# Row-major attention and mixing weights halved by DMA in a two-layer encoder

## The chip, the cores and the metric

The kernel runs on one core of one Trainium2 chip. The metric is the device time of one execution in microseconds (us), as the median of several runs. A core has five engines with a queue each: TensorE (PE, matrix products into PSUM banks), VectorE (DVE), ScalarE (ACT), GpSimd (POOL) and SyncE (SP, which here only issues DMAs). A queue is worked off in order; an instruction that waits for another engine holds up all behind it.

## The reference

Two layers on 512 tokens of width 1024, all in float32. Each layer mixes tokens in two ways side by side and then runs a gated MLP:

```python
h = rmsnorm(x, g_mix[l]); z = h @ w_in[l]
q, k, v, x_rec, gate = jnp.split(z, [512, 1024, 1536, 2048], axis=-1)
att = neighbourhood_attention(q, k, v, rel_bias[l])    # 8 heads of 64, tokens on an 8 x 64 grid
xc = depthwise_conv(x_rec, ...)                         # width 4
rec_f = rg_lru(xc, ..., reverse=False); rec_b = rg_lru(xc, ..., reverse=True)
rec = (rec_f + rec_b) * gelu(gate, approximate=True)
x = x + concat([rmsnorm(att, g_att[l]), rmsnorm(rec, g_rec[l])]) @ w_out[l]
u_act, u_lin = split(rmsnorm(x, g_ffn[l]) @ w_up[l])
x = x + (gelu(depthwise_conv(u_act, ...)) * u_lin) @ w_down[l]
```

A query at grid column c sees all 8 rows and a window of 16 columns, with a learned bias per head. `rg_lru` makes two gates r and i by 64-wide block products and sigmoids, a = exp(-8 r softplus(-lam)), and scans h = a h + sqrt(1 - a^2) i x over the tokens. A last rmsnorm ends the program.

## The kernel before

Activations lie transposed: 128 channels on the partitions, 512 tokens along them. Each weight is read from memory once, in chunks of 128 x 1024 (eight 128 x 128 blocks, 512 KB), in the order that `weight_plan` lists. Every operand of these products is split into a rounded high half and a low half, and `mm3` (L187 to L190) issues three products: high by high, low by high, high by low. A column of `w_in` (128 outputs) is eight blocks, 24 matmuls of 512 columns.

A weight chunk passes three steps. `load_to` has SP load it into `raw` (2 buffers). `split_to` has ACT copy it rounded to `hi` (L171, 4 buffers) and DVE subtract, `lo = raw - hi` (L172, 4 buffers). `chunk` hands it to the products and calls the two others for chunks further on (3 ahead for the split, 6 for the load).

The mixing stage of a layer starts with the recurrent input columns, a group of four banks (`xr`). Then the string `MIX` (L43) sets the order in which the program's steps are written, and with it TensorE's order: `q`, `k`, `v`, `g` followed by a number are the four columns of queries, keys, values and the gate branch (an `a` or `b` behind it is a half of one); `c` is the convolution of a channel tile; `t` the recurrent gates of a tile, with exponentials, a square root and the two scans (`lru_gates`, L469); `S`, `T` and `P` are scores and softmax, transposes of the weights, and products with the values, each for half the columns of a pair of heads, so numbers 0 to 7; `u` transposes values to token order and copies their halves, shifted by half a tile, into two `edge` tiles (POOL, L564); `o` and `n` are output products and norms. A scheduler sets the order of the other engines: by its own estimate of when things are ready, with what stands under `urgent()` first.

Queries, keys and values are stored column by column of the grid (`by_column`), so DVE writes or reads them in strides when it evacuates a bank (L528, L536, L547). `query_tile` (L509) keeps two tiles per pair with zeros from POOL. The gate branch computes its GeLU by hand, ACT square, three DVE steps, ACT tanh (`gate_tile`, L573), within the step that makes the column. PSUM has eight banks: three for columns (`ps_mm`), two for scores, two for transposes, one for products (`ps_o`).

After the stage come the output products and the MLP: per tile two columns of `w_up`, a convolution and a GeLU from ACT's table (L771), then `w_down`.

## Time and profile before

| what | value |
|---|---|
| three runs | 1230.93 us median, 1230.6 to 1231.04 |
| profiled execution | 1230.33 us, its span 1228.5 us |
| PE busy | 1201.5 us (98%) |
| DVE busy | 791.6 us (64%) |
| ACT busy | 488.0 us (40%) |
| POOL busy | 46.3 us (4%) |
| granted TensorE clock | 0.998 of full |

The span counts from the first instruction to the last; busy time is the union of an engine's instructions. Matmuls overlap, and their ends are modelled, so PE's share says less than its steps from one matmul to the next. By the names in the timeline the mixing stages lie at about 26 to 218 us and 631 to 823 us; MLP parts fill the rest.

### The profile page before, as it was taken

How to read it: one execution, taken by the hardware profiler on the slowest of the kernel's cores; microseconds unless marked ns; L12 is line 12 of the kernel's file. 1: busy time of each engine (PE TensorE's matmuls, PEld its weight loads, DVE VectorE, ACT ScalarE, POOL GpSimd, SP SyncE). 2: the span in 40 equal slices, each digit the busy share in tenths (PEclk: the TensorE clock that was granted, in tenths of full speed). 3: DMA queues.
4: the chain of work that ended last, by engine and by line, in shares of the span. 5: the costliest groups of instructions: out<-in, count | busy, mean ns of one | idle time of the engine just before them, and what ended most of it. 6: DMA issues, size and time to landing. Idle time of an engine off the chain costs nothing.

```text
span 1228.5 us, 14279 instructions
## 1 busy us (share of the span) xinstructions
PE 1201.5 (98%) x5566; PEld 991.2 (81%) x5566; DVE 791.6 (64%) x1257; ACT 488.0 (40%) x717; POOL 46.3 (4%) x88
## 2 busy tenths in 40 slices
PE   9999999999999999999999999999999999999997
PEld 7777778888888888888887777788888888888886
DVE  8999876865544455553659998677555255565454
ACT  6687534433221232332429765344323212223220
POOL 2001010000000000000010011100000000000000
PEclk9999999999999999999999999999999999999999
DMA  7222213223223223233222221142332322322322
GB/s 239 81 69 93 84 35 103 90 99 103 91 98 103 87 101 103 88 102 103 86 86 77 77 86 52 35 137 87 103 93 96 103 91 98 103 87 101 103 69 69
DMA packets 34355, 114.06 MB, mean 93 GB/s; under 512 B 3825, under 2 KB 7025, under 8 KB 34289
## 3 DMA queue, kind: packets, MB, share of 16 engines
q1 hardware_dynamic: 34144, 113.17, 28.1%
q8 instruction: 43, 0.70, 0.2%
q14 instruction: 24, 0.19, 0.0%
q10 hardware_dynamic: 144, 0.00, 0.0%
HBM read 111.06 MB, written 2.10 MB: 92 GB/s over the span
## 4 chain that ended last, share of the span: by engine, by line
PE 78%; DVE 11%; ACT 4%; issue 2%; DMA 1%; POOL 0%; POOLq 0%; DVEq 0%; ACTq 0%
PE dn L188 7%; PE dn L190 7%; PE dn L189 7%; PE pl L188 6%; PE pa L188 6%; PE pa L189 6%; PE pl L189 6%; PE pa L190 6%; PE pl L190 6%; PE out L188 2%; PE out L190 2%; PE out L189 2%; DVE lo L172 2%; PE up L188 1%; PE up L190 1%
## 5 line engine op out<-in xcount | busy, mean ns | idle before, releaser
L171 ACT ACTIVATE hi<-raw 128x1024 fp32r<-128x1024 f32 (+1 forms) x205 | 216.3, 1055 | 452.9 <-PE dn L189 156.6
L172 DVE TENSOR_TENSOR lo<-raw,hi 128x1024 fp32r<-128x1024 f32 (+1 forms) x205 | 249.6, 1218 | 142.9 <-ACT hi L171 142.4
L763 DVE TENSOR_TENSOR ua<-pa,g_ffn_rb 128x512 f32<-128x512 f32 x44 | 30.4, 691 | 112.9 <-PE pa L190 112.9
L771 ACT ACTIVATE uc<-uc,cols 128x512 f32<-128x512 f32 x48 | 34.8, 724 | 129.7 <-DVE uc L769 129.6
L772 DVE TENSOR_TENSOR uc<-pl,uc 128x512 f32<-128x512 f32 x44 | 30.4, 691 | 73.5 <-PE pl L190 72.0
L740 DVE TENSOR_TENSOR dns<-dn,g_ffn_rb 128x512 f32<-128x512 f32 x30 | 20.4, 689 | 29.4 <-PE dn L190 29.4
L769 DVE SCALAR_TENSOR_TENSOR uc<-ua,cols,uc 128x511 f32<-128x511 f32 x48 | 36.0, 751 | 1.5
L767 DVE SCALAR_TENSOR_TENSOR uc<-ua,cols,uc 128x511 f32<-128x511 f32 x48 | 35.8, 745 | 0.1
L628 ACT ACTIVATE prob<-prob,mx 128x192 f32<-128x192 f32 (+1 forms) x64 | 27.5, 431 | 12.0 <-DVE mx L626 11.9
L615 PEld LDWEIGHTS s<-k,q 128*128 128x128 f32 x128 | 19.6, 190 | 8.8 <-issue 4.2
L188 PE MATMUL out<-atth,hi 128*128 128x512 f32 x64 | 26.1, 407 | 0.4 <-ACT atth L684 0.4
L615 PE MATMUL s<-k,q 128*128 128x192 f32 (+1 forms) x128 | 23.2, 324 | 3.2 <-DVE mx L622 1.4
L190 PE MATMUL out<-atth,lo 128*128 128x512 f32 x64 | 25.4, 397 | 0.0
L189 PE MATMUL out<-attl,hi 128*128 128x512 f32 x64 | 25.3, 396 | 0.0
L766 DVE TENSOR_SCALAR uc<-ua,cols 128x512 f32<-128x512 f32 x48 | 23.4, 487 | 1.5
L517 POOL MEMSET q<- 64x256 f32 x32 | 10.0, 311 | 367.4 <-PE dn L189 366.1
L679 DVE COPY att<-o 64x256 f32<-64x256 f32 x32 | 19.6, 612 | 4.6 <-PE o L190 4.1
L528 DVE TENSOR_TENSOR q<-qps,g_mix_rb 64x256 f32<-64x256 f32 x32 | 20.6, 644 | 0.4
L741 DVE TENSOR_TENSOR x<-x,dns 128x512 f32<-128x512 f32 x30 | 20.1, 687 | 0.4
L622 DVE CUSTOM_DVE_ANT_0 prob<-s,bias 128x192 f32<-128x192 f32 (+1 forms) x64 | 18.2, 338 | 1.8 <-PE pte L649 0.6
L564 POOL CAST edge<-vh 64x384 fp32r<-64x384 f32 x16 | 9.4, 591 | 254.5 <-ACT vh L559 254.0
L458 DVE SCALAR_TENSOR_TENSOR xc<-xrs,cols,xc 128x511 f32<-128x511 f32 (+1 forms) x24 | 17.9, 747 | 0.4
(930 smaller groups left out, 3547.4 us busy)
## 6 DMA issues: line engine op xcount, KB each, us to landing
raw<-in_w SPq DMA_DIRECT2D x203, 512.0 KB, 3.5
x<-in_x SPq DMA_DIRECT2D x8, 256.0 KB, 5.1
out_y<-out SPq DMA_DIRECT2D x8, 256.0 KB, 2.3
bias<-in_bias SPq DMA_DIRECT2D x8, 224.0 KB, 2.5
raw<-in_w SPq DMA_DIRECT2D x2, 256.0 KB, 3.1
cols<-in_cols SPq DMA_DIRECT2D x1, 164.0 KB, 5.0
cols<-in_cols ACTq DMA_DIRECT2D x1, 4.0 KB, 3.0
```

What stands on the lines that cost most here:

```text
L171: nc.scalar.activation(hi[:, sl], raw[:, sl], AF.Copy)
L172: nc.vector.tensor_tensor(out=lo[:, sl], in0=raw[:, sl], in1=f32(hi[:, sl]), op=ALU.subtract)
L188: nc.tensor.matmul(ps, a[0], b[0], start=start, stop=False)
L189: nc.tensor.matmul(ps, a[0], b[1], start=False, stop=False)
L190: nc.tensor.matmul(ps, a[1], b[0], start=False, stop=stop)
L615: nc.tensor.matmul(ps[:, o:o + ROWS * w], qt[:, b % 4 * P:(b % 4 + 1) * P], kt[:, ROWS * kc0:ROWS * (kc0 + w)], start=True, stop=True)
L628: nc.scalar.activation(pr[b], pr[b], AF.Exp, bias=mx[:, b % 4:b % 4 + 1], accum_out=sm[:, b % 4:b % 4 + 1])
L763: nc.vector.tensor_tensor(out=ua, in0=pa, in1=rbf[0], op=ALU.mult)
L767: nc.vector.scalar_tensor_tensor(out=c[:, 1:], in0=ua[:, :T - 1], scalar=w[0], in1=c[:, 1:], op0=ALU.mult, op1=ALU.add)
L769: nc.vector.scalar_tensor_tensor(out=c[:, :T - 1], in0=ua[:, 1:], scalar=w[2], in1=c[:, :T - 1], op0=ALU.mult, op1=ALU.add)
L771: nc.scalar.activation(c, c, AF.Gelu_apprx_tanh, bias=col("conv_ffn_b", j, l))
L772: nc.vector.tensor_tensor(out=c, in0=pl_, in1=c, op=ALU.mult)
```

## The change

Four things change together.

- **Layout.** Queries, keys and values stay in row order within groups of 8 grid columns (`by_group`), the bias table is laid out to match on the host, and the scores' moving operand is read through a pattern of runs of 8. The two query tiles per pair become one constant tile `q_pair` whose zeros are written once.
- **Weights.** For the mixing stage's columns and gate chunks (`by_dma`), POOL issues a DMA that rounds the weights into `hi`; ACT writes `lo = -hi`; POOL issues a second DMA that adds the weights to `lo`. Loads run at most 3 chunks ahead and splits 2. The recurrent input columns, `w_out` and the MLP keep the old way.
- **Order.** `MIX` is written anew: a pair's gates, convolution and scans come with its heads instead of all at the front, gates in two halves inside the keys' column, values before scores. A gate chunk now holds one tile (half width, 256 KB), so a layer's stage has 20 chunks by DMA, where 18 stood.
- **Gate branch.** One table GeLU on ACT, in a step `e` of its own, and one product.

`p_w2` goes to one buffer, and the softmax steps stand under `urgent()` one by one.

```diff
@@ -40,9 +40,11 @@
 
 
 
-MIX = ("q0 c0 c1 k0 t0 k1 q1 c2 t1 q2 k2 c3 t2 k3 q3 S0 v0a T0 t3 v0b g0a v1a S1 u0 P0 "
...
+
+MIX = ("q0 c0 k0a t0a k0b t0b v0a S0 v0b S1 g0a c1 u0 g0b T0 q1a q1b P0 T1 c2 k1a t1a k1b P1 t1b "
+       "v1a e0 S2 v1b S3 g1a u1 c3 g1b T2 q2a q2b P2 T3 k2a t2a k2b P3 t2b "
...
 IN_TILE = {"q": 0, "k": 4, "v": 8, "g": 16}
 
 
...
@@ -59,9 +61,8 @@
 
         pairs("w_in", 0, 8, [12, 13, 14, 15])
         for step in MIX:
-            if step in ("t0", "t0a", "t2", "t2a"):
-                t = int(step[1])
-                plan.append(("gate", l, [(t + a, dg) for a in range(2) for dg in range(4)]))
+            if step[0] == "t" and step[-1] != "b":
+                plan.append(("gate", l, [(int(step[1]), dg) for dg in range(4)]))
             elif step[0] in IN_TILE and step[-1] != "b":
                 column("w_in", IN_TILE[step[0]] + int(step[1]))
         for m in range(0, 8, 2):
...
@@ -142,16 +143,31 @@
         return tc.high_priority(offset=level * URGENT) if level else ExitStack()
 
 
-    raws, halves = {}, {}
+    raws, highs, halves = {}, {}, {}
     state = {"load": 0, "split": 0, "use": 0}
     AHEAD_LOAD, AHEAD_SPLIT = 6, 3
 
     def pieces(i):
         return (slice(0, 1024),) if i else (slice(0, 512), slice(512, 1024))
+
+    def width(i):
+        return P * len(plan[i][2])
+
+    def by_dma(i):
+
+        w, _, bs = plan[i]
+        return w == "gate" or w == "w_in" and bs[0][1] != 12
 
     def load_to(n):
         while state["load"] < min(n, len(plan)):
             i = state["load"]
+            if by_dma(i):
+                if i > state["use"] + 3:
+                    return
+                highs[i] = p_hi.tile([P, 1024], F32R, tag="hi", name=f"hi{i}")
+                nc.gpsimd.dma_start(highs[i][:, :width(i)], w_d[i][:, :width(i)])
+                state["load"] += 1
+                continue
             raws[i] = p_raw.tile([P, 1024], F32, tag="raw", name=f"raw{i}")
             for n, sl in enumerate(pieces(i)):
                 nc.sync.dma_start(raws[i][:, sl], w_d[i][:, sl])
...
@@ -162,7 +178,19 @@
     def split_to(n):
         while state["split"] < min(n, len(plan)):
             i = state["split"]
+            if by_dma(i) and i > state["use"] + 2:
+                return
             load_to(i + 1)
+            if i in highs:
+                hi = highs.pop(i)
+                lo = p_lo.tile([P, 1024], F32R, tag="lo", name=f"lo{i}")
+                with urgent(1):
+                    ws = slice(0, width(i))
+                    nc.scalar.activation(lo[:, ws], f32(hi[:, ws]), AF.Copy, scale=-1.0)
+                    nc.gpsimd.dma_start(lo[:, ws], w_d[i][:, ws], accum_op=ALU.add)
+                halves[i] = (hi, lo)
+                state["split"] += 1
+                continue
             raw = raws.pop(i)
             hi = p_hi.tile([P, 1024], F32R, tag="hi", name=f"hi{i}")
             lo = p_lo.tile([P, 1024], F32R, tag="lo", name=f"lo{i}")
...
@@ -337,11 +370,11 @@
             return r
 
 
-    def by_column(ap):
-        return ap.rearrange("p (c r) -> p r c", r=ROWS)
-
-    def by_row(ap):
-        return ap.rearrange("p (r c) -> p r c", r=ROWS)
+    def by_group(ap):
+        return ap.rearrange("p (r g c) -> p g r c", r=ROWS, c=8)
+
+    def in_group(ap):
+        return ap.rearrange("p g (r c) -> p g r c", r=ROWS)
 
     def by_head(ap):
         return ap.rearrange("p (j h t) -> p j h t", h=2, t=64)
...
@@ -477,7 +510,7 @@
                 ti = big(p_t, "t", f"ti{l}{t}{d}")
                 for g, o in ((0, w), (1, ti)):
                     ps = psum(ps_o if d and g and not o_ps[0] else ps_mm, f"gp{l}{t}{d}{g}")
-                    mm3(ps, blk(c, 4 * (t % 2) + 2 * d + g), xcs[t], True, True)
+                    mm3(ps, blk(c, 2 * d + g), xcs[t], True, True)
                     i = ((l * 2 + d) * 2 + g) * 4 + t
                     with urgent():
                         nc.scalar.activation(o, ps, AF.Tanh, scale=0.5, bias=half_b[:, i:i + 1])
...
@@ -507,34 +540,20 @@
         qk = {}
 
         def query_tile(i):
-
-            qk[i] = [big(p_h, "h", f"q{l}{i}{n}") for n in range(2)]
-
-            def zones(other):
-                return [by_head(t[64 * a:64 * a + 64])[:, :, a ^ other] for t in qk[i] for a in (0, 1)]
-
-            for z in zones(1):
-                nc.gpsimd.memset(z, 0.0)
             ps = psum(ps_mm, f"qps{l}{i}")
             yield from column_parts(ps, "w_in", l, i, xg, 4)
             with urgent():
-                for n, z in enumerate(zones(0)):
-                    rows = slice(64 * (n % 2), 64 * (n % 2) + 64)
-                    cs = slice(32 * (n // 2), 32 * (n // 2) + 32)
-
-                    def grid(ap):
-                        return by_row(ap)[rows, :, cs].rearrange("p r (j c) -> p r j c", c=8)
-
-                    nc.vector.tensor_tensor(out=z.rearrange("p j (c r) -> p r j c", r=ROWS), in0=grid(ps),
-                                            in1=grid(rb), op=ALU.mult)
+                for n in range(2):
+                    rows = slice(64 * n, 64 * n + 64)
+                    nc.vector.tensor_tensor(out=in_group(q_pair[rows, :, n]), in0=by_group(ps)[rows],
+                                            in1=by_group(rb)[rows], op=ALU.mult)
 
         def key_tile(i):
             ps = psum(ps_mm, f"kps{l}{i}")
             yield from column_parts(ps, "w_in", l, 4 + i, xg, 4)
             qk[4 + i] = big(p_h, "h", f"k{l}{i}")
             with urgent():
-                nc.vector.scalar_tensor_tensor(out=by_column(qk[4 + i]), in0=by_row(ps), scalar=0.125,
-                                               in1=by_row(rb), op0=ALU.mult, op1=ALU.mult)
+                nc.vector.scalar_tensor_tensor(out=qk[4 + i], in0=ps, scalar=0.125, in1=rb, op0=ALU.mult, op1=ALU.mult)
 
 
         v = [None] * 4
...
@@ -570,19 +590,19 @@
         recs = [None] * 4
         atts = [None] * 4
 
+        branch = [None] * 4
+
         def gate_tile(t):
             ps = psum(ps_mm, f"gate{l}{t}")
             yield from column_parts(ps, "w_in", l, 16 + t, xg, 4)
-            z = big(p_t, "t", f"z{l}{t}")
+            branch[t] = big(p_t, "t", f"z{l}{t}")
             with urgent():
-                nc.vector.tensor_tensor(out=z, in0=ps, in1=rb, op=ALU.mult)
-            s = big(p_t, "t", f"zs{l}{t}")
-            nc.scalar.activation(s, z, AF.Square)
-            nc.vector.tensor_scalar(out=s, in0=s, scalar1=0.044715, scalar2=1.0, op0=ALU.mult, op1=ALU.add)
-            nc.vector.tensor_tensor(out=s, in0=s, in1=z, op=ALU.mult)
-            nc.scalar.activation(s, s, AF.Tanh, scale=math.sqrt(2.0 / math.pi))
-            nc.vector.scalar_tensor_tensor(out=z, in0=s, scalar=1.0, in1=z, op0=ALU.add, op1=ALU.mult)
-            nc.vector.scalar_tensor_tensor(out=fb[t], in0=fb[t], scalar=0.5, in1=z, op0=ALU.mult, op1=ALU.mult)
+                nc.vector.tensor_tensor(out=branch[t], in0=ps, in1=rb, op=ALU.mult)
+
+        def gate_end(t):
+            z = branch[t]
+            nc.scalar.activation(z, z, AF.Gelu_apprx_tanh)
+            nc.vector.tensor_tensor(out=fb[t], in0=fb[t], in1=z, op=ALU.mult)
             rec_stats.add(fb[t])
 
         def finish_rec():
...
@@ -602,7 +622,7 @@
 
         def scores(h):
             blocks = range(4 * (h % 2), 4 * (h % 2) + 4)
-            bt, qt, kt = bias[h // 2], qk[h // 2][h % 2], qk[4 + h // 2]
+            bt, kt = bias[h // 2], by_group(qk[4 + h // 2])
             pr = {}
             st_ = probs_of[h % 2]
             mx = p_s.tile([P, 4], F32, tag="mx", name=f"mx{l}{h}")
...
@@ -612,25 +632,27 @@
                 o = 0
                 for b in pair:
                     kc0, w, _ = BLOCKS[b]
-                    nc.tensor.matmul(ps[:, o:o + ROWS * w], qt[:, b % 4 * P:(b % 4 + 1) * P],
-                                     kt[:, ROWS * kc0:ROWS * (kc0 + w)], start=True, stop=True)
+                    nc.tensor.matmul(ps[:, o:o + ROWS * w], q_pair[:, b], kt[:, kc0 // 8:(kc0 + w) // 8],
+                                     start=True, stop=True)
                     c0 = 0 if b % 2 else 2 * P - ROWS * w
                     pr[b] = st_[:, b % 4, c0:c0 + ROWS * w], ps[:, o:o + ROWS * w]
                     o += ROWS * w
```

Three places in the order. First POOL's queue in layer 0 behind the setup. Before, it holds zeros for queries (`q`), the root for the norm, and the values' edge copies:

```order
L327 TENSOR_TENSOR g_mix_r<-g_mix_ms,expo 128x4 [waits DVE_49,Pool_49]
L517 MEMSET q_594 64x4x64
L517 MEMSET q_594 64x4x64 [waits Pool_49]
L517 MEMSET q_595 64x4x64 x2
L517 MEMSET q_688 64x4x64 x2
L517 MEMSET q_689 64x4x64 x2
L517 MEMSET q_854 64x4x64 x2
L517 MEMSET q_855 64x4x64 x2
L564 COPY edge_159<-vh_1078 64x384 [waits Activation_49]
L564 COPY edge_159<-vh_1078 64x384
L564 COPY edge_160<-vl_1079 64x384 [waits DVE_49]
L564 COPY edge_160<-vl_1079 64x384
```

Now, around the first pair's values (`hi` and `lo` are weight chunks: hi_689 and lo_760 v1, hi_763 and lo_777 g1, hi_780 and lo_862 q2, hi_865 and lo_944 k2):

```order
L168 DMA hi_689<-in_w 128x1024 [waits DMASW0_49,PE_49]
L190 DMA lo_760<-in_w 128x1024 [waits DMASW1_49,PE_49,Activation_49]
L584 COPY edge_159<-vh_646 64x384 [waits Activation_49]
L584 COPY edge_159<-vh_646 64x384 [waits Pool_49]
L584 COPY edge_160<-vl_647 64x384 [waits DVE_49]
L584 COPY edge_160<-vl_647 64x384
L168 DMA hi_763<-in_w 128x1024 [waits DMASW2_49,PE_49]
L190 DMA lo_777<-in_w 128x1024 [waits DMASW3_49,DMASW4_49,PE_49,Activation_49]
L168 DMA hi_780<-in_w 128x1024 [waits PE_49]
L168 DMA hi_865<-in_w 128x1024 [waits DMASW6_49,DMASW5_49,PE_49]
L190 DMA lo_862<-in_w 128x1024 [waits Activation_49]
```

The edge copies stand between weight DMAs; each `lo` waits for ACT, each `hi` for TensorE to leave the buffer of four chunks earlier.

Second, ACT in layer 0. Before, around one square root (`w`) of a gate tile and the values' high half (`vh`):

```order
L171 ACTIVATE hi_1014<-raw_924 128x1024 [waits DMAHW1_49,PE_49]
L487 ACTIVATE w_955<-w_955,sp 128x512 [waits Activation_49]
L489 ACTIVATE a_988<-a_985 128x512
L495 ACT_TABLE_LOAD
L495 ACTIVATE w_955<-w_955 128x1024 [waits DVE_49]
L559 ACTIVATE vh_1078<-vtp_1073 128x512 [waits PE_49]
L653 ACTIVATE pt_1111<-ptw_1102 128x512
L171 ACTIVATE hi_1033<-raw_1018 128x1024 [waits DMAHW2_49,PE_49]
L653 ACTIVATE pt_1113<-pte_1103 128x384 [waits Activation_49]
```

Now, from the second scores of the second pair (`prob_158`) to its products (hi_947 and lo_1015 are the next gate chunk, hi_1018 and lo_1080 the next values):

```order
L189 ACTIVATE lo_1015<-hi_947 128x512 [waits DMASW1_49,DMASW0_49,PE_49]
L528 ACT_TABLE_LOAD
L528 ACTIVATE w_782<-w_782 128x1024 [waits DVE_49]
L650 ACT_TABLE_LOAD
L650 ACTIVATE prob_158,sm_922<-prob_158,mx_921 128x192 [waits DVE_49]
L650 ACTIVATE prob_158,sm_922<-prob_158,mx_921 128x192 x2
L650 ACTIVATE prob_158,sm_922<-prob_158,mx_921 128x128
L579 ACTIVATE vh_966<-vtp_961 128x512 [waits PE_49]
L676 ACTIVATE pt_1006<-ptw_997 128x512 [waits PE_49]
L604 ACT_TABLE_LOAD
L604 ACTIVATE z_995<-z_995 128x512 [waits DVE_49]
L676 ACTIVATE pt_1008<-pte_998 128x384 [waits PE_49]
```

The negated copy of the next gate chunk stands ahead of the root, and root, exponentials and GeLU each have a table load ahead.

Third, DVE at the same place. Before, the scans (`fb`, `w`) of that tile with the values' low half and the transposed weights:

```order
L497 TENSOR_TENSOR ti_956<-ti_956,w_955 128x512 [waits Activation_49]
L560 TENSOR_TENSOR vl_1079<-vtp_1073,vh_1078 128x512 [waits Activation_49,Pool_49]
L500 SCALAR_TENSOR_TENSOR fb_994<-a_967,ti_956 128x512 [waits DVE_49]
L497 TENSOR_TENSOR ti_974<-ti_974,w_955 128x512
L503 SCALAR_TENSOR_TENSOR w_955<-a_985,ti_974 128x512 [waits DVE_49]
L679 COPY att_1099<-o_1086 64x32x8 [waits PE_49]
L505 TENSOR_TENSOR fb_994<-fb_994,w_955 128x512 [waits DVE_49]
L654 TENSOR_TENSOR pt_1112<-ptw_1102,pt_1111 128x512 [waits Activation_49]
L172 TENSOR_TENSOR lo_1034<-raw_1018,hi_1033 128x1024 [waits DMAHW2_49,PE_49,Activation_49]
L654 TENSOR_TENSOR pt_1114<-pte_1103,pt_1113 128x384 [waits Activation_49]
```

Now:

```order
L530 TENSOR_TENSOR ti_783<-ti_783,w_782 128x512 [waits Activation_49]
L530 TENSOR_TENSOR ti_836<-ti_836,w_782 128x512 [waits DVE_49]
L600 TENSOR_TENSOR z_995<-gate_943,g_mix_rb 128x512 [waits PE_49]
L533 SCALAR_TENSOR_TENSOR fb_856<-a_794,ti_783 128x512 [waits DVE_49]
L536 SCALAR_TENSOR_TENSOR w_782<-a_847,ti_836 128x512 [waits DVE_49]
L652 RECIPROCAL sm_922<-sm_922 128x4 [waits Activation_49]
L538 TENSOR_TENSOR fb_856<-fb_856,w_782 128x512 [waits DVE_49]
L654 TENSOR_SCALAR prob_158<-prob_158,sm_922 128x192 [waits DVE_49]
L654 TENSOR_SCALAR prob_158<-prob_158,sm_922 128x192 x2
L654 TENSOR_SCALAR prob_158<-prob_158,sm_922 128x128
L580 TENSOR_TENSOR vl_967<-vtp_961,vh_966 128x512 [waits Activation_49]
L677 TENSOR_TENSOR pt_1007<-ptw_997,pt_1006 128x512 [waits Activation_49]
```

The weight subtraction (`lo<-raw,hi`) and the attention copies left this stretch; the gate branch and the softmax's normalisation (`prob_158`) stand in it.

## Rows read from the trace of the kernel before

**Rows 1.** Windows: both mixing stages and part of an MLP; columns as the second line says.

```profile
core 0: us, PE busy (x) PEld busy (x) DVE busy (x) ACT busy (x) POOL busy (x), PEclk, DMA share, GB/s
25.60:217.80 192.20, 183.78 (x895) 148.06 (x894) 165.56 (x326) 112.71 (x201) 14.41 (x26) 1.00 0.26 82
300.00:400.00 100.00, 100.00 (x443) 82.81 (x442) 48.26 (x60) 26.58 (x29) 0.00 (x0) 1.00 0.29 97
631.00:823.10 192.10, 183.53 (x898) 148.57 (x897) 163.48 (x314) 113.59 (x202) 15.96 (x29) 1.00 0.23 77
```

**Rows 2.** TensorE's waits, whole span (waiter, releaser, us, times, longest); one MLP matmul row.

```profile
PE ptw L645 <- DVE pt L654: 3.8, 6, 1.5
...
PE o L190 <- POOL edge L564: 3.2, 6, 1.1
...
PE o L188 <- DVE att L679: 2.3, 4, 0.7
...
PE ptw L645 <- DVE prob L632: 1.5, 2, 0.8
...
L188 PE MATMUL pa<-xg_g_ffn_0h,hi 128*128 128x512 f32 x44 | 17.1, 389 | 0.0
```

**Rows 3.** Groups by line, VectorE, 25 to 220 us (busy us, mean ns, idle before).

```profile
L172 DVE TENSOR_TENSOR lo<-raw,hi 128x1024 fp32r<-128x1024 f32 x28 | 34.3, 1225 | 7.9 <-ACT hi L171 7.6
...
L528 DVE TENSOR_TENSOR q<-qps,g_mix_rb 64x256 f32<-64x256 f32 x16 | 10.3, 642 | 0.2
...
L547 DVE TENSOR_TENSOR vt<-vps,g_mix_rb 128x512 f32<-128x512 f32 x4 | 4.7, 1171 | 0.4 <-PE vps L190 0.4
...
L536 DVE SCALAR_TENSOR_TENSOR k<-kps,g_mix_rb 128x512 f32<-128x512 f32 x4 | 4.5, 1134 | 0.0
...
L578 DVE TENSOR_TENSOR z<-gate,g_mix_rb 128x512 f32<-128x512 f32 x4 | 2.7, 679 | 0.5 <-PE gate L190 0.5
```

**Rows 4.** Groups by line, ScalarE, 25 to 220 us.

```profile
L171 ACT ACTIVATE hi<-raw 128x1024 fp32r<-128x1024 f32 x28 | 29.6, 1056 | 36.7 <-DMA raw<-in_w 9.1 <-PE qps L189 6.9 <-PE gate L189 6.2
...
L495 ACT ACT_TABLE_LOAD x4 | 5.1, 1283 | 0.1
...
L495 ACT ACTIVATE w<-w 128x1024 f32<-128x1024 f32 x4 | 4.2, 1062 | 1.1 <-DVE w L490 1.1
...
L580 ACT ACTIVATE zs<-z 128x512 f32<-128x512 f32 x4 | 2.5, 625 | 4.1 <-DVE z L578 4.1
```

**Rows 5.** The page's groups: the MLP's GeLU.

```profile
L771 ACT ACTIVATE uc<-uc,cols 128x512 f32<-128x512 f32 x48 | 34.8, 724 | 129.7 <-DVE uc L769 129.6
```

**Rows 6.** Chain of waits, 45 to 100 us (start us, us, what).

```profile
50.18 1.81 ACT prob L628 x8
...
52.22 0.96 DVE prob L632 x4
...
77.90 1.11 DVE ti L497 x2
...
79.01 1.13 DVE fb L500
...
80.14 1.11 DVE w L503
...
89.39 0.66 PE ptw L645 x4
...
92.68 1.20 PE s L615 x8
```

**Rows 7.** Groups by line, POOL, 0 to 220 us.

```profile
L564 POOL CAST edge<-vl 64x384 fp32r<-64x384 f32 x8 | 5.5, 689 | 3.2 <-DVE vl L560 2.7
...
L327 POOL TENSOR_TENSOR g_mix_r<-g_mix_ms,expo 128x4 f32<-128x4 f32 x1 | 1.0, 1025 | 17.6 <-DVE sp_q L280 17.6
```

**Rows 8.** The page's DMA issues: weights in one and in two pieces.

```profile
raw<-in_w SPq DMA_DIRECT2D x203, 512.0 KB, 3.5
...
raw<-in_w SPq DMA_DIRECT2D x2, 256.0 KB, 3.1
```

More of the change, by code (lines that the diff above doesn't have):

```diff
@@ L112, in encoder @@
     p_fb = pool("p_fb", 4)
-    p_w2 = pool("p_w2", 2)
+    p_w2 = pool("p_w2", 1)
     p_t = pool("p_t", 12)
@@ L256, in encoder @@
         nc.gpsimd.memset(f32(t[64:P, 0:P]), 0.0)
+    q_pair = const.tile([P, 8, 2, 64], F32, name="q_pair")
+    nc.gpsimd.memset(q_pair[64:P, :, 0], 0.0)
+    nc.gpsimd.memset(q_pair[0:64, :, 1], 0.0)
     NL = 16
@@ L469, in lru_gates @@
         def lru_gates(t, ds):
-            if t % 2 == 0 and 0 in ds:
+            if 0 in ds:
                 pair["c"] = chunk("gate", l, (t, 0))
@@ L621, in scores @@
                     _, w, bo = BLOCKS[b]
[L622 to L624 removed]
+                    with urgent():
+                        nc.vector.tensor_tensor_reduce(out=pr[b][0], in0=pr[b][1], in1=bt[:, bo:bo + ROWS * w],
+                                                       scale=1.0, scalar=-3e38, op0=ALU.add, op1=ALU.max,
+                                                       accum_out=mx[:, b % 4:b % 4 + 1])
                     pr[b] = pr[b][0]
[L626 to L633 removed]
+            with urgent():
+                nc.vector.tensor_scalar(out=mx, in0=mx, scalar1=-1.0, scalar2=None, op0=ALU.mult)
+                for b in blocks:
+                    nc.scalar.activation(pr[b], pr[b], AF.Exp, bias=mx[:, b % 4:b % 4 + 1],
+                                         accum_out=sm[:, b % 4:b % 4 + 1])
+                nc.vector.reciprocal(sm, sm)
+                for b in blocks:
+                    nc.vector.tensor_scalar(out=pr[b], in0=pr[b], scalar1=sm[:, b % 4:b % 4 + 1], scalar2=None,
+                                            op0=ALU.mult)
             return st_
@@ L652, in transposes @@
             for t, src, cs in ((t1, whole, slice(0, T)), (t2, part, sl)):
-                nc.scalar.activation(t[0][:, cs], src[:, cs], AF.Copy)
-                nc.vector.tensor_tensor(out=t[1][:, cs], in0=src[:, cs], in1=f32(t[0][:, cs]), op=ALU.subtract)
+                with urgent():
+                    nc.scalar.activation(t[0][:, cs], src[:, cs], AF.Copy)
+                    nc.vector.tensor_tensor(out=t[1][:, cs], in0=src[:, cs], in1=f32(t[0][:, cs]), op=ALU.subtract)
             return t1, t2
@@ L676, in products @@
                 rows = slice(64 * a, 64 * a + 64)
-                dst = by_row(at)[rows, :, 32 * (h % 2):32 * (h % 2) + 32].rearrange("p r (j c) -> p j c r", c=8)
-                src = by_head(o)[rows, :, a].rearrange("p j (c r) -> p j c r", r=ROWS)
-                nc.vector.tensor_copy(dst, src)
+                with urgent():
+                    nc.vector.tensor_copy(by_group(at)[rows, 4 * (h % 2):4 * (h % 2) + 4],
+                                          by_head(o)[rows, :, a].rearrange("p j (r c) -> p j r c", r=ROWS))
             if h % 2:
@@ L723, in layer @@
                     nc.sync.dma_start(bias[n // 2], bias_d[l, n // 2])
-                with urgent():
-                    probs[n] = scores(n)
+                probs[n] = scores(n)
             elif what == "T":
-                with urgent():
-                    turned[n] = transposes(n, probs.pop(n))
+                turned[n] = transposes(n, probs.pop(n))
             elif what == "P":
@@ L867, in lay_out @@
     rel = a["rel_bias"]
-    bias = np.full((L, H, 8, ROWS, NBIAS), MASKED, np.float32)
+    bias = np.full((L, H, ROWS, 8, NBIAS), MASKED, np.float32)
     for q0, (kc0, w, bo) in ((0, BLOCKS[0]), (8, BLOCKS[1]), (56, BLOCKS[7])):
-        part = bias[..., bo:bo + ROWS * w].reshape(L, H, 8, ROWS, w, ROWS)
+        part = np.full((L, H, ROWS, 8, ROWS, w), MASKED, np.float32)
         for qr in range(ROWS):
```

28 lines of the change are left out of this document (10 added, 18 removed).

## Prediction

> **What bounds the kernel now.** I read three stretches of the window view first [rows 1]. In the MLP stretch, 300 to 400 us, TensorE is never idle: 443 matmuls in 100 us, 0.226 us each, at the full granted clock (the 2.4 GHz level). Nothing off TensorE can make that part faster, and the change doesn't touch it. The two mixing stages differ: TensorE is idle 192.2 - 183.8 = 8.4 us in the first and 192.1 - 183.5 = 8.6 us in the second. A record lasts longer than the step to the next one (0.389 us on a row of the MLP's matmuls against 0.226), so every gap shows about 0.16 us short [rows 1, 2]; the four largest wait rows count 18 gaps, I take 28 for all, and the loss is about 17.0 + 4.5 = 21.5 us. **That is all the change can win.** VectorE (DVE) is the engine that TensorE waits for there: 165.6 us of 192.2 busy [rows 1], and the waits of TensorE name it, or GpSimd (POOL) copies that start after it: pt 3.8, edge 3.2, att 2.3, prob 1.5 us [rows 2].
>
> **What the change takes off DVE and ScalarE (ACT).** Per layer, from mean durations of rows. Weights: the low half of 18 mixing chunks (16 columns, 2 gate chunks) is no longer subtracted: 18 x 1.225 = 22.1 us off DVE. Queries: four strided products of 0.642 become two over all columns, priced like the gate's 128x512 product, 0.679: 4 x (2.57 - 1.36) = 4.8. Keys and values stay in row order: 4 x (1.134 - 0.68) + 4 x (1.171 - 0.68) = 3.8. GeLU in one table function: per tile three DVE steps of at most a product's 0.68 go: some 7. In all 38 us less: DVE falls from 165.6 to about 128 us of 192 [rows 1, 3]. ACT loses 18 high halves and eight 0.625 us steps (24.0) and gets 16 negated copies at 1.056, four half-wide ones at 0.58, four GeLUs at 0.72 and, by the order of its instructions, 32 table loads in place of 20, so six more per layer at 1.283: 29.8. It ends at about 118 us instead of 112.7 [rows 1, 4, 5]. TensorE's matmuls are the same in number. The 16 query memsets per layer leave POOL; they hid in its idle time, as it is busy 14.4 us of 192 [rows 1].
>
> **What it adds.** Each of the 20 mixing chunks per layer is now a load issued by POOL that rounds, an ACT copy with the sign turned, and a second POOL DMA that adds the original. ACT stands still in its queue until the first has landed; POOL stands still until ACT has copied; behind that wait in POOL's queue stand the edge copies of the values, for which TensorE waits in the products. No row of before shows a rounding or adding DMA. Bounds: plain SP loads land 3.5 us (512 KB) and 3.1 us (256 KB) after issue [rows 8]; nothing in the trace makes the new ones quicker, so that is the low end. The high end is twice that, 7.0 and 6.2, since the adding one must read two streams, and the rounding one might go at half rate. I take 4.5 and 4.0: the plain row plus 1.0 us of POOL's own, the price of POOL's smallest real operation (four columns, 1.025) [rows 7]. The low end seems nearer because DMA engines are only 26% busy in the stage [rows 1].
>
> The DMA page of the Trainium skill (DMA: Bandwidth & Descriptors, section Anatomy of one DMA) puts a POOL-issued DMA at about 2.0 us plus its bytes at 436 GB/s, an estimate of 3.2 us for 512 KB, for plain copies; no run here shows it yet. By that figure the sum below would end near 1215 us.
>
> **Is a column's weight late?** Between two uses of a buffer (four each for high and low halves) lie three chunks on TensorE, 17 to 22 us in a pair of heads of 31.6. The two DMAs and the copy take 4.5 + 1 to 3 + 4.5, about 12. So weights themselves arrive in time, even at 7 us each (17, just). What is late is the rest of ACT's queue.
>
> **The chain that now ends last, walked by the new order.** Zero is the end of a pair's second transposes. TensorE, at 0.226 us a matmul: half a column 2.7, one direction's gates 1.4, products 1.4 (12 of half width), scores 1.2, transposes 0.7 to 1.0 [rows 1, 6]. So k ends at 6.8, the second gates at 9.6, the second half of v at 16.3, the next pair's odd scores at 17.5, g at 23.4, transposes at 24.1, the next q at 29.5, and there the even head's products should start. Against it: the load of the next gate chunk waits for v's buffer, so it is issued at 16.3 and lands at 20.3. ACT's negated copy of it stands before the square root: copy 0.5, table load 1.3, root 1.0 (of 1024 columns), table load 1.3: 24.4; four exponentials 1.8, then the values' high half, the transposed weights' copy, another table load, GeLU, second copy, to about 29.4 [rows 4 to 6]. DVE goes on from the root at 23.1: products 1.1, gate branch 0.6, two scans 1.1 each, sum 0.6, four normalisations 1.0, values' low half 0.6, low half of the transposed weights 0.6, and after a convolution step the second one: 30.1 and 31.0 [rows 3, 6]. TensorE wants the first at 29.5 and the second 0.4 later: it waits about 1.4 us. Middle pairs, two per layer: 1.4 each.
>
> First pair, walked the same way from the start of its q: ACT copies the weight of g before it clears the gates' second bank, so the reverse gates start about 0.8 late. At its first products the values' evacuation stands on ACT behind a GeLU table load and the copy of v's next chunk, whose load can start only when g has left its buffer (at 28.2; landed 32.7, copied 33.7, values 34.8); the four edge copies, up to 0.69 each [rows 7], end near 37.2, where TensorE wanted them at 34.8: about 2.4. Last pair: no mixing weights follow, 0.5. Together 0.8 + 2.4 + 2.8 + 0.5 = 6.5 us per layer, 13 in two, against 21.5. The gain is 8.5 us.
>
> The start of layer 1 gives nothing: the reciprocal root for the rows stands on POOL behind two weight DMAs and comes some 0.6 us late, where before 0.4 was lost on the same spot. The tail of the stage, the w_out part and both MLPs keep their instructions.
>
> Sum: the profiled execution is 1230.3 us (span 1228.5 and 1.8 around it), the median 0.6 more. 1230.9 - 8.5 = 1222.4; I say 1222.
>
> The SBUF page of the Trainium skill (SBUF — State Buffer, on DVE blocking DMA) warns that some DVE operations lock POOL out while it writes the descriptors of its DMAs. Of the kinds it names, the trace has the four normalisations, 1.0 us in a run [rows 6]. By that rule the load at 16.3 could start up to 1 us later; eight pairs at 1 us would leave the kernel at about 1230, the case "no gain" below.
>
> **Rivals.** (1) *Landings are quick, as plain loads are.* 3.5 and 3.1 us: each late chain comes 1 us earlier, the middle pairs wait 0.4, the first 2.2, 3.5 per layer; 1230.9 - 14.5 = 1216. For it: an idle DMA system. Against: POOL must do something per DMA. (2) *POOL's DMAs land late and ACT's in-order queue hands that to TensorE.* Place: ACT's copy of the next gate chunk ahead of the square root. Price: seven of the eight pairs have such a chain, so each us of landing beyond 4 costs 7 us; above 4.0 + 8.5 / 7 = 5.2 us the gain is gone; at 7 us the kernel takes 1222 + 21 = 1243. For it: rounding and adding are shown in no row, and six more table loads per layer leave ACT no slack in that chain. Against: lookahead of two to three chunks. (3) *No gain*: landings near 5 us, or 1 us of lost POOL time per pair: 1229 to 1232. (4) *The scores' moving operand* is now read in runs of 8 elements. DVE pays for such patterns (keys 1.134 against 0.68, 1.66 times) [rows 3]; TensorE's 64 score matmuls at the same factor would cost 1.2 x 16 x 0.66 = 12.7 us, all on its path: 1235. A row of TensorE with such a pattern there is none; I bound it by 0 and 12.7 and take 0, as each score block already takes longer per column than a product (four blocks in 1.2 us) and so may hide it.
>
> **Chances.** Forecast, 1216 to 1227: 0.45. Rival 1: 0.13. Rival 3: 0.14. Rival 2: 0.22. Rival 4: 0.06. A measurement of this kernel can tell 0.2%, 2.5 us, from no change. Faster: 0.45 + 0.13 less a little = 0.56; within 0.2%: 0.12; slower: 0.32. The range for 8 in 10 goes from 1209 (all waits gone, 1230.9 - 21.5) to 1243, the late landings; the forecast's own is 1216 to 1227.
>
> **What would show it.** The median landing of the POOL DMAs (4.0 to 4.5 forecast); DVE near 128 us in each mixing stage, ACT near 118; TensorE's idle time there falling from 17 to about 10 us, with "o" waiting for pt and edge as the largest rest; the score matmuls still 1.2 us per head. Wrong would be: landings above 5.2 us, with ACT idle before the negated copies and "gp" or "o" waiting in turn; TensorE waiting for lo itself; longer score matmuls.

## The result and the profile after

The changed kernel takes 1249.45 us (median of 4 runs) against 1230.95: a ratio of 1.0157 over all runs, 95% interval 1.0142 to 1.0172 (the two medians alone give 1.0150), 18.5 us slower. The forecast was 1222, in a range of 1209 to 1243.

The windows of the changed kernel, for the stages of [rows 1]: from a stage's first norm to its last output product, as there. They last 200.7 and 200.9 us in place of 192.2 and 192.1:

```profile
core 0: us, PE busy (x) PEld busy (x) DVE busy (x) ACT busy (x) POOL busy (x), PEclk, DMA share, GB/s
26.00:226.70 200.70, 188.26 (x897) 157.06 (x898) 129.00 (x279) 121.33 (x207) 38.03 (x53) 0.96 0.50 119
300.00:400.00 100.00, 100.00 (x442) 82.80 (x442) 50.31 (x63) 26.77 (x30) 0.00 (x0) 1.00 0.30 95
640.80:841.70 200.90, 186.03 (x897) 155.41 (x898) 128.96 (x280) 122.23 (x208) 39.06 (x54) 0.97 0.50 118
```

DVE lost the work that it was to lose, and TensorE got nothing from it: it stands still for longer, and in places its granted clock is below 1. The MLP is as before. The three largest of TensorE's waits (waiter, releaser, us, times, longest); [rows 2] named pt, edge, att and prob, of which pt and prob are left with 1.4 and 0.8 us:

```profile
PE o L217 <- ACT lo L189: 9.9, 4, 2.9
PE o L216 <- ACT vh L579: 8.1, 2, 5.4
PE s L635 <- DVE mx L643: 1.8, 1, 1.8
```

Fewer waits, but longer. The first two rows are waits ahead of a head pair's first products; their releasers stand at the end of a chain that began elsewhere. The DMA issues (KB each, median us to landing) beside [rows 8], and ACT's group of negated copies from the page:

```profile
raw<-in_w SPq DMA_DIRECT2D x167, 512.0 KB, 3.4
hi<-in_w POOLq DMA_DIRECT2D x32, 512.0 KB, 5.2
lo<-in_w POOLq DMA_DIRECT2D x32, 512.0 KB, 5.5
...
hi<-in_w POOLq DMA_DIRECT2D x8, 256.0 KB, 5.5
lo<-in_w POOLq DMA_DIRECT2D x8, 256.0 KB, 4.1
```

```profile
L189 ACT ACTIVATE lo<-hi 128x1024 fp32r<-128x1024 f32 (+1 forms) x40 | 38.9, 972 | 78.3 <-DMA hi<-in_w 38.9 <-issue 20.8 <-PE vtp L575 6.7
```

ACT stood still for 78.3 us ahead of 40 copies, 38.9 of it by name for a load. The chain of waits over one of these places, the second head pair of layer 0:

```profile
94.32 0.23 PE vps L218
...
98.50 0.45 PE vtp L575 x4
98.96 1.60 issue
100.55 0.63 ACT lo L189
...
101.20 1.28 ACT L528
102.50 1.06 ACT w L528
...
103.58 1.28 ACT L650
...
105.67 1.01 ACT prob L650 x5
106.68 0.48 ACT vh L579
107.17 0.48 ACT pt L676
107.66 1.28 ACT L604
...
110.96 0.58 PE o L217
```

The time lines of POOL, ACT, DVE and TensorE there (start, us, what, idle before):

```profile
90.73 0.88 POOL L190 DMA_DIRECT2D lo<-in_w  x1 [2.25 <-ACT lo L189]
93.05 0.88 POOL L190 DMA_DIRECT2D lo<-in_w  x1 [1.44 <-ACT lo L189]
94.62 0.57 POOL L168 DMA_DIRECT2D hi<-in_w  x1 [0.70 <-PE vps L218]
```

```profile
100.55 0.63 ACT L189 ACTIVATE lo<-hi 128x512 fp32r<-128x512 f32 x1 [4.35 <-issue]
```

```profile
103.59 1.29 DVE L530 TENSOR_TENSOR ti<-ti,w 128x512 f32<-128x512 f32 x2 [5.64 <-ACT w L528]
...
110.23 0.67 DVE L677 TENSOR_TENSOR pt<-ptw,pt 128x512 fp32r<-128x512 f32 x1
```

```profile
110.96 0.58 PE L217 MATMUL o<-pt,vh 128*128 128x256 f32 x1 [2.88 <-ACT lo L189]
```

Read from POOL on: the gate chunk's load is issued at 94.62, when TensorE's last v matmul has freed its buffer, 1.6 us behind an adding DMA and 3.9 behind another. It lands 5.9 us later, at 100.5. Most of that it spends in the queue: of its packets in the trace (2048 bytes each) the first starts at 98.16, 3.5 us after the issue, as the last of the adding DMAs' start (98.1 to 98.3). A load with nothing ahead of it on the queue (issued at 85.17) has its first packet after 1.25 us and lands in 3.8, though it is twice as large. Until the landing ACT stands still, for 4.35 us; the square root, the exponentials and the values stand behind the copy, and DVE is idle for 5.64 us until the root comes. The second products (L217) start at 110.96, after 2.88 us of idle TensorE. They need the low half of pt, which DVE ends at 110.90; the waits view put this wait down to lo, an ACT copy that ended just then as well. What ACT lost here was not made up behind it.

The first pair of layer 1, with the longest wait (5.4 us), shows a second way to be late. Its gate chunk's load was issued at 671.69, straight behind two adding DMAs (669.49 and 671.14), the second of which had waited in POOL's queue for ACT's copy; it landed 6.6 us later, and ACT stood still for 5.28 us. Of the 40 loads, 12 start like this, within 0.7 us behind an adding DMA with POOL not idle between them: ACT waits for a load, an adding DMA waits for ACT, and the next load stands behind it.

Then the clock. Three of the six stretches in which it fell inside the stages (30.7 us in all; before had none):

```profile
72.70:79.50 6.80, 6.68 (x24) 5.91 (x25) 5.85 (x10) 2.15 (x3) 2.23 (x5) 0.50 0.61 149
110.20:117.00 6.80, 6.02 (x23) 5.45 (x24) 6.63 (x13) 2.17 (x4) 2.64 (x4) 0.50 0.61 137
687.10:693.90 6.80, 5.10 (x21) 4.62 (x22) 5.49 (x10) 2.73 (x5) 4.16 (x6) 0.50 0.40 92
```

0.50 is the 1.2 GHz level. TensorE had waited 2.7, 2.9 and 5.4 us at the start of these stretches or just ahead. The books, from TensorE's records between the start and 1185 us: idle gaps between matmuls 17.2 us before, 28.9 after (+11.7); the steps of matmuls inside the six slow stretches, against the same at full clock, +12.4; the rest, small delays of matmuls that are no gap, -5.3, taken as the remainder. The sum, 18.8, is what TensorE's last record came later (1222.1 to 1240.9).

### The profile page after: what moved, and what is told of

Its sections match the earlier page's. It is cut to its first block, busy times and chain, and to the rows that moved or that the text cites. A ratio compares the mean times of both kernels' runs of the same rounds, so it can differ in the third digit from the quotient of the medians.

```text
span 1247.6 us, 14243 instructions
## 1 busy us (share of the span) xinstructions
PE 1208.6 (97%) x5566; PEld 1006.1 (81%) x5566; DVE 716.2 (57%) x1181; ACT 500.9 (40%) x725; POOL 95.4 (8%) x138
## 3 DMA queue, kind: packets, MB, share of 16 engines
q1 hardware_dynamic: 28960, 94.29, 23.4%
q0 software_dynamic: 11520, 37.75, 13.9%
## 4 chain that ended last, share of the span: by engine, by line
PE 83%; issue 5%; DVE 5%; DMA 3%; ACT 2%; POOL 1%; SPq 0%; POOLq 0%; DVEq 0%; ACTq 0%
PE pl L217 6%; PE pl L218 6%; PE pa L218 6%; PE pa L217 6%; PE pa L216 6%; PE pl L216 6%; PE dn L218 6%; PE dn L217 6%; PE dn L216 6%; DMA hi<-in_w 2%; PE out L218 2%; PE out L216 2%; PE out L217 2%; PE up L216 1%; PE up L218 1%
## 5 line engine op out<-in xcount | busy, mean ns | idle before, releaser
L199 ACT ACTIVATE hi<-raw 128x1024 fp32r<-128x1024 f32 (+1 forms) x169 | 178.2, 1055 | 400.4 <-PE dn L217 159.8
L200 DVE TENSOR_TENSOR lo<-raw,hi 128x1024 fp32r<-128x1024 f32 (+1 forms) x169 | 205.5, 1216 | 134.7 <-ACT hi L199 134.4
L795 DVE TENSOR_TENSOR uc<-pl,uc 128x512 f32<-128x512 f32 x44 | 30.4, 692 | 73.4 <-PE pl L218 71.8
L189 ACT ACTIVATE lo<-hi 128x1024 fp32r<-128x1024 f32 (+1 forms) x40 | 38.9, 972 | 78.3 <-DMA hi<-in_w 38.9
L168 POOL DMA_DIRECT2D hi<-in_w x40 | 26.6, 682 | 420.6 <-PE xr L218 391.1
L190 POOL DMA_DIRECT2D lo<-in_w x40 | 35.1, 877 | 148.2 <-ACT lo L189 129.2
L524 DVE SCALAR_TENSOR_TENSOR ti<-ti,xc 128x512 f32<-128x512 f32 x16 | 11.0, 688 | 25.7 <-ACT ti L516 25.7
L217 PE MATMUL out<-attl,hi 128*128 128x512 f32 x64 | 25.2, 393 | 0.0
L530 DVE TENSOR_TENSOR ti<-ti,w 128x512 f32<-128x512 f32 x16 | 10.6, 688 | 25.2 <-ACT w L528 25.2
L789 DVE TENSOR_SCALAR uc<-ua,cols 128x512 f32<-128x512 f32 x48 | 23.4, 487 | 1.6
L635 PE MATMUL s<-k,q_pair 128*128 128x192 f32 (+1 forms) x128 | 22.0, 314 | 1.8 <-DVE mx L643 1.8
L635 PEld LDWEIGHTS s<-k,q_pair 128*128 128x128 f32 x128 | 20.8, 190 | 3.4 <-DVE mx L643 2.1
```

Of the source, the lines that this page charges most:

```text
L189: nc.scalar.activation(lo[:, ws], f32(hi[:, ws]), AF.Copy, scale=-1.0)
L190: nc.gpsimd.dma_start(lo[:, ws], w_d[i][:, ws], accum_op=ALU.add)
L199: nc.scalar.activation(hi[:, sl], raw[:, sl], AF.Copy)
L200: nc.vector.tensor_tensor(out=lo[:, sl], in0=raw[:, sl], in1=f32(hi[:, sl]), op=ALU.subtract)
L217: nc.tensor.matmul(ps, a[0], b[1], start=False, stop=False)
L635: nc.tensor.matmul(ps[:, o:o + ROWS * w], q_pair[:, b], kt[:, kc0 // 8:(kc0 + w) // 8], start=True, stop=True)
```

## The experiments

All times stand beside the kernel before, run on the same chip (1230.7 to 1231.2). The theory, A: the load of a high half is issued late, ACT stands in its queue for it ahead of the values, and TensorE pays in waits and in clock.

**One part undone, and the adding left out.** The first gives the weights their halves the old way (a second line, in `pieces`, lets SP load a gate chunk at its own width):

```
 def by_dma(i):
-    return w == "gate" or w == "w_in" and bs[0][1] != 12
+    return False
```

> One part undone: the mixing weights are halved as before (load by SP, high half on ACT, low half on DVE); the new order, the row-major layout, the gates in two halves and the GeLU table stay. Theory A (ACT stands in its queue for a POOL load that lands late, the values behind it come late, TensorE waits in its products and its granted clock then falls to half): no ACT instruction of the two mixing stages waits for a landing over 1 us, the 2.9 and 5.5 us waits ahead of the first products go, the 31 us at half clock go, DVE is back at 135 to 145 us busy per stage, and the time is 1222 to 1233 us. Rival B (the new order with its table loads between values and probabilities costs the time itself): the products wait as long as now and the time stays at 1243 to 1251 us. Rival C (DMA traffic of the two POOL queues slows the rest): as A in time, but then also the run in which only the adding is left out stays slow.

Measured: 1208.97 us, ratio 0.982 (0.9805 to 0.9835), 13 us below A's range, which had given the new order no gain of its own. DVE is at 148 and 146 us in the two stages, a little over what A said; no stretch of them is at half clock, and the largest wait for values is small:

```profile
PE o L216 <- ACT vh L579: 0.7, 1, 0.7
```

So order, layout and GeLU together are worth 22 us, not a loss; rival B falls. In the second, the copy on ACT and the adding go:

```
-    nc.scalar.activation(lo[:, ws], f32(hi[:, ws]), AF.Copy, scale=-1.0)
-    nc.gpsimd.dma_start(lo[:, ws], w_d[i][:, ws], accum_op=ALU.add)
+    nc.gpsimd.dma_start(lo[:, ws], w_d[i][:, ws])
```

> The negated copy on ACT is left out and the second DMA converts the weight again instead of adding it, so the low half holds the rounded weight and not the remainder; the number and size of the DMAs and their queue stay. Theory A: no ACT instruction waits for a landing any more, so ACT reaches the values in time, the waits ahead of the products and the half clock go, and the time is 1218 to 1232 us. Rival B (order and table loads): 1243 to 1251 us. Rival C (the POOL queue and the DMA traffic themselves): 1240 us or more, with TensorE waiting for weight halves by name. If the adding itself were the cost (a slow read and write back of the low half), the landings of the second DMA fall from 5.5 to about 3.5 us as well.

Measured: 1204.74 us, ratio 0.9786 (0.977 to 0.9802), again 13 us below A's range: as many bytes on POOL's queue, and no loss. The run leaves out the copy and the adding together, so it does not say which of the two does the harm, and the queue takes less of the DMA engines' time (9.8% against 13.9). Against rival C the runs with a fifth buffer, below, weigh more: there the adding stays. The DMA issues:

```profile
hi<-in_w POOLq DMA_DIRECT2D x32, 512.0 KB, 3.8
lo<-in_w POOLq DMA_DIRECT2D x32, 512.0 KB, 4.5
...
lo<-in_w POOLq DMA_DIRECT2D x8, 256.0 KB, 3.3
hi<-in_w POOLq DMA_DIRECT2D x8, 256.0 KB, 2.9
```

The second DMA lands in 4.5, not in the 3.5 named for a slow adding. With no adding on the queue a rounding DMA lands in 2.9 to 4.5 us, by the medians. In the changed kernel it depends on what is queued: its 19 loads of 512 KB that were issued with an adding DMA on its way landed in 5.7 us (median), the 13 others in 4.2.

**The load earlier, in two ways.** A fifth buffer for high halves, paid for with two work buffers; first also asked for one chunk sooner, then only the buffers, then only the price:

```
-    p_t = pool("p_t", 12)          # all three
+    p_t = pool("p_t", 10)
-    p_hi = pool("p_hi", 4)         # first and second
+    p_hi = pool("p_hi", 5)
-    if i > state["use"] + 3:       # first
+    if i > state["use"] + 4:
```

> The high half is issued one chunk earlier (five buffers in place of four, paid for with two work buffers of ten), the adding DMAs and the negated copies stay. Theory A: the gate chunk's load is issued one chunk earlier, 6 us or more ahead of now, so its negated copy on ACT waits under 1 us in place of 4.4, the first products of each pair wait under 1.5 us in place of 2.9 to 5.5, and most of the 31 us at half clock go: 1222 to 1235 us. Rival B (order and table loads): no change, 1246 to 1252 us. Rival D (the low half's adding DMA, issued behind the copy, is what comes too late): TensorE waits for low halves by name and the time stays over 1240 us.

> Five buffers of high halves and ten work buffers as in the run with the load one chunk earlier (1205.3 us), but the load is asked for at the same chunk as in the changed kernel; with the spare buffer its issue waits for TensorE's chunk before the last and no longer for the one just done, and it stands ahead of an adding DMA in POOL's queue. Theory A (what counts is how early the high half lands ahead of its negated copy on ACT): the issue comes 3 to 6 us earlier, ACT's waits for landings fall from 38.9 to under 15 us, and the time is 1206 to 1225 us. Rival F (only the chunk at which it is asked for counts, not the buffer): 1243 to 1252 us.

> The changed kernel with ten work buffers in place of twelve, nothing else: the price paid for the earlier load, alone. Theory A: 1246 to 1256 us, no gain. Rival G (the smaller pool moved the order and made the gain of the earlier load): 1200 to 1235 us.

Measured: 1205.33 us (ratio 0.9796, 0.9781 to 0.981), 1205.66 (0.9795, 0.9779 to 0.9811) and 1249.15 (1.0157, 1.014 to 1.0173). Against the changed kernel's 1249.45 the buffer alone is worth 43.8 us; the smaller pool did nothing, asking sooner added nothing. Both times are below A's ranges, the first by 17 us, the second by less than 1. With the buffer only, the DMA issues and ACT's group from the page:

```profile
hi<-in_w POOLq DMA_DIRECT2D x32, 512.0 KB, 4.3
lo<-in_w POOLq DMA_DIRECT2D x32, 512.0 KB, 6.5
...
hi<-in_w POOLq DMA_DIRECT2D x8, 256.0 KB, 5.9
lo<-in_w POOLq DMA_DIRECT2D x8, 256.0 KB, 4.8
```

```profile
L189 ACT ACTIVATE lo<-hi 128x1024 fp32r<-128x1024 f32 (+1 forms) x40 | 38.7, 967 | 20.8 <-PE xr L218 14.7 <-PE qps L218 3.0 <-PE gate L218 1.3
```

Of the landings only those of the 512 KB loads are shorter (5.2 to 4.3); the gate chunks' (5.5 to 5.9) and the low halves' are longer, and ACT waits 1.3 us in all for loads ahead of these copies, where it was 38.9. So the spare buffer, and with it the earlier issue, is enough, though the gate chunk itself takes longer to land. Whether a shorter landing at the old issue would be enough too was not run. TensorE's longest wait in the stages is 0.8 us, and it waits for no low half by name (rival D). Now 3 loads of the 40, not 12, start straight behind an adding DMA. The same gate chunk here, on POOL and on ACT:

```profile
75.24 0.87 POOL L190 DMA_DIRECT2D lo<-in_w  x1 [1.06 <-ACT lo L189]
76.38 0.56 POOL L168 DMA_DIRECT2D hi<-in_w  x1 [0.27 <-PE gp L218]
79.17 0.87 POOL L190 DMA_DIRECT2D lo<-in_w  x1 [2.23 <-ACT lo L189]
```

```profile
83.45 0.63 ACT L189 ACTIVATE lo<-hi 128x512 fp32r<-128x512 f32 x1
84.10 1.28 ACT L528 ACT_TABLE_LOAD   x1
...
89.49 0.57 ACT L579 ACTIVATE vh<-vtp 128x512 fp32r<-128x512 f32 x1
```

It waits for the chunk before v (gp) and not for v, and stands ahead of one of the adding DMAs: issued at 76.38, 14.3 us ahead of the first q matmul of the next pair (90.70); in the changed kernel 7.6 us (94.62 and 102.25). It lands at 82.2, and the copy starts at 83.45 with ACT never idle. Whether the earlier release or the place ahead of an adding DMA does more was not separated: the spare buffer brings both.

**The copy on another engine, the gates the old way.** First `nc.gpsimd.tensor_scalar(... scalar1=-1.0 ...)` in place of the negated copy on ACT; then `by_dma` without `w == "gate"`:

> The negated copy runs on POOL in place of ACT; loads, adding DMAs, buffers and order stay, so the high halves land as late as now. Theory A (ACT's queue carries the wait into the values): ACT waits for no landing, the values come in time, the waits of 2.7 to 5.4 us ahead of the first products fall under 1.5 us, and the time is 1206 to 1235 us; the price is POOL, which copies 40 times at 1 to 4 us each and holds the edge copies and the next loads behind its own wait. Rival D (late low halves stop TensorE, on whatever engine they are negated): TensorE waits for low halves by name and the time stays over 1243 us.

> Only the eight gate chunks go the old way (load by SP, high half on ACT, low half on DVE); the 32 chunks of the other mixing weights keep their converting and adding DMAs. Theory A with the gate chunk as the culprit (its 256 KB load is queued behind two adding DMAs just ahead of the square root and the values): the waits ahead of the first products fall under 1.5 us, and the time is 1208 to 1228 us. Rival H (every chunk is late alike, whichever stands ahead of the values): the time stays at 1236 to 1252 us.

Measured: 1288.69 us (ratio 1.0472, 1.0456 to 1.0488), and 1218.92 (0.9906, 0.9892 to 0.9921). On POOL, its group and TensorE's waits:

```profile
L189 POOL TENSOR_SCALAR lo<-hi 128x1024 fp32r<-128x1024 f32 (+1 forms) x40 | 106.2, 2655 | 137.3 <-issue 64.5 <-DMA hi<-in_w 59.6 <-PE pte L671 9.5
```

```profile
PE o L216 <- POOL edge L584: 22.7, 4, 10.4
PE qps L218 <- DMA lo<-in_w: 13.0, 4, 3.8
PE gate L218 <- DMA lo<-in_w: 8.7, 5, 2.1
```

A's range was missed by over 50 us, by the price that it named: a copy takes 2.7 us there in the mean, and behind its wait stand the edge copies and the loads. The wait for the landing went into another in-order queue, with worse behind it. What rival D named, TensorE waiting for low halves by name, did come in this run (25.1 us in the three rows with `lo<-in_w`; one of them not shown); with the copies on ACT no such row stands in the changed kernel. With the eight gate chunks out of the way, 30.5 of the 43.8 us come back, though ACT still waits 44.3 us for the other loads and two waits of 2.0 and 2.2 us are left where A said under 1.5. So ACT's waits in sum do not measure the loss. It fits that a wait costs where something urgent is behind it, which for the gate chunk is the square root and the values; the run changes SP's, ACT's and DVE's work on these chunks as well, so it does not prove that.

**The products later.** `k1a`, `k2a` and `k3a` of the order stand ahead of `P0`, `P2` and `P4`:

> The changed kernel with one edit in its order: in each head pair half a key column (12 matmuls, 2.7 us by their steps) stands ahead of the first head's products and no longer behind both heads' scores; four buffers as now. Theory A (the loads are issued when TensorE is done with a chunk, the products come too soon behind): TensorE has 2.7 us more to do before each of the six late products, so waits of 2.7 to 5.4 us fall by up to 2.7 us each, some 10 to 14 us, and with them a part of the 31 us at half clock: 1222 to 1240 us, not as fast as the spare buffer (1205.7 us), since ACT still waits for its landings (38.9 us). Rival J (the wait follows the chunk wherever it is placed): 1244 to 1254 us.

Measured: 1243.93 us (ratio 1.0112, 1.0092 to 1.0133): 5.5 us won, at the lower edge of J and short of A. The waits ahead of the products fell (the L217 row from 9.9 to 2.8 us), but ACT's waits for loads rose from 38.9 to 55.2; the chunks had moved with the products.

**The old order.** Before's code with the weights' halves by DMA and nothing else, with four and with five high buffers:

> One part alone: the kernel before, with its order, its column-major scores, its gates in pairs of branches and its GeLU by square and tanh, and only the halves of the mixing weights made by converting and adding DMAs. Theory A: ACT stands in its queue for late landings here too (over 20 us idle in front of its negated copies), so that what DVE saves is not won and the time is 1230 to 1255 us. Rival B (the DMAs are cheap and the order costs): DVE's 13 us less per stage are won and the time is 1216 to 1228 us.

> The kernel before with its order, layout and GeLU, the mixing weights by converting and adding DMAs, and a fifth buffer of high halves (ten work buffers in place of twelve). With four it took 1250.9 us. Theory A (the load's issue, held for a buffer until TensorE is done with a chunk, made the loss in either order): ACT's waits for landings fall from 51.6 to under 20 us, the 17 us at half clock go, and the time is 1215 to 1232 us. Rival K (the loss belongs to the DMAs in this order, with its chunks of two branches' gates): 1240 to 1252 us.

Measured: 1250.85 us (ratio 1.016, 1.0145 to 1.0176) and 1229.83 (0.999, 0.998 to 0.9999), both in A's ranges. ACT's group with four, then with five:

```profile
L188 ACT ACTIVATE lo<-hi 128x1024 fp32r<-128x1024 f32 x36 | 38.0, 1056 | 66.0 <-DMA hi<-in_w 51.6 <-issue 9.1 <-PE o L217 4.0
```

```profile
L188 ACT ACTIVATE lo<-hi 128x1024 fp32r<-128x1024 f32 x36 | 38.0, 1055 | 33.6 <-PE xr L217 13.6 <-PE gate L217 7.8 <-DMA hi<-in_w 6.9
```

**The old GeLU** (square, tanh and three more DVE steps) in the run with the old halves:

> The new order and layout with the halves made the old way (1209.0 us) and, besides, the old GeLU by square and tanh in place of the GeLU function of ACT: three more DVE instructions per branch, 0.6 to 1.2 us each, some 12 us per stage, and no load of the GeLU's table. Theory A (order and room for DVE give the gain; the GeLU decides little): 1208 to 1218 us. Rival B (the table loads between values and probabilities cost): under 1206 us.

Measured: 1210.91 us (ratio 0.9841, 0.9824 to 0.9857), 1.9 us over that run; the GeLU decides little, and no cost of its table loads shows here.

Put together, with TensorE's idle gaps and its time at half clock, both up to 1190 us (before's order with its layout and GeLU; the new ones together; five buffers with the smaller work pool):

| halves of the weights | before's order: us, gaps, half clock | new order: us, gaps, half clock |
|---|---|---|
| by ACT and DVE | 1231.0, 17.2, 0 | 1209.0, 4.0, 0 |
| DMA, four high buffers | 1250.9, 30.2, 17.1 | 1249.5, 28.9, 30.7 |
| DMA, five high buffers | 1229.8, 16.2, 3.4 | 1205.7, 2.4, 0 |

With four buffers the DMAs cost 20 us in the one order and 40 in the other; with five they bring 1 (hardly clear of noise) and 3. The version to keep is the new order with five buffers: 25 us under before.

## Why the prediction was wrong

- **DVE and ACT: right.** DVE at about 128 us: 129.0 in both stages. ACT at about 118: 121.3 and 122.2. Rival 4 was wrong: the score matmuls take 314 ns in the mean, 324 before.
- **The chain: right in its place and order.** The load at v's end, the copy ahead of the root, the table loads, then DVE's row of steps up to pt: each stands in the trace of a middle pair where the walk put it. Rival 2 named this place, and the sign of being wrong (landings above 5.2 us, ACT idle ahead of its copies) is what came.
- **"I take 4.5 and 4.0": the failing term.** The landings were 5.2, 5.5 and 5.5 us in the median, and 5.9 for the gate chunk shown. They were priced as single transfers on DMA engines with time to spare; in the trace the gate chunk's load stands behind two adding DMAs of 512 KB and moves its first packet 3.5 us after its issue. With no adding on the queue loads landed in 3.8 (512 KB) and 2.9 (256 KB), below the forecast. Middle pairs waited 2.8 us in the mean in place of 1.4; the walk itself gives 3.3 with 5.9 put in.
- **The first pairs were undersized.** 3.2 us forecast; 6.3 in layer 0 (1.4, 1.8, 2.7 and 0.3 in four gaps) and 8.3 in layer 1 (1.4, 0.7, 5.4, 0.8), where the gate chunk's load came straight behind adding DMAs and the values stand on ACT behind a GeLU and its table load as well. Together the gaps were 28.9 us against the 13 of the sum (which counted each gap 0.16 us longer than the trace shows it).
- **The clock had no term at all.** 12.4 us. "Each us of landing beyond 4 costs 7 us" priced waits at their length; behind some of them the matmuls ran at 1.2 GHz too. By rival 2's own formula, 5.5 to 5.9 us would have been 1232 to 1235. Gaps (28.9 - 13 = 15.9) and clock (12.4) together make 28.3 us, about the whole way from 1222 to 1249.
- **"Weights themselves arrive in time": true, and the wrong question.** No weight was late for TensorE by name in the changed kernel; they were late for ACT's copy. And the landing was taken as the quantity that decides, while the run with the spare buffer shows that an earlier issue cures the loss though the gate chunk lands no faster (5.9 us): the prediction saw that the load waits for v's buffer and took that as given.
- **"All the change can win" (21.5 us) was a little low:** the new order won 22 without the DMAs and 25 with five buffers.
- **Two slips in the working changed little.** The walk's figures give a middle pair 31.0 - 29.9 = 1.1 us of wait, not 1.4. And prob (1.5 us) is not the fourth largest wait before: one of 1.7 us, of `gp` for k, is larger.
- **What the Trainium skill said.** The formula of the Trainium skill (DMA: Bandwidth & Descriptors, Anatomy of one DMA; an estimate of 3.2 us for 512 KB) comes near the rounding DMA without adding (3.8) and is 2 us short of the changed kernel's median (5.2). The Trainium skill (DMA: Bandwidth & Descriptors, Two DMAs through the same engine are not ordered) says that within one queue of a DMA engine descriptors start in order. The first packet at 98.16, behind those of two adding DMAs, agrees. Of the locking by DVE that the Trainium skill describes (SBUF — State Buffer, SBUF: two separate sides) nothing shows at the place weighed: POOL began the load at 94.62, 0.07 us after the matmul that released it, and its first packet followed the adding DMAs'; no run isolates the lock.

What stays open: how much of the spare buffer's gain is the earlier release and how much the place ahead of an adding DMA; whether faster landings alone would do; and when the clock falls: a gap of 2.7 us was followed by a fall in the changed kernel (71.8 us) and by none in the old order with four buffers (663 us).
